# Where the weight sums of three streamed Strassen products are made: in DRAM ahead of each product, or in the product's own SBUF tile

## The chip, the cores and the metric

The kernel runs on one core of a Trainium2 chip. The metric is device microseconds of one execution; before the change the median of three is 1978.28 us (1976.78 to 1981.49). The profile comes from one further execution, which took 1979.15 us, 1977.4 of them from its first to its last instruction.

## The reference

One decoder block on 1024 tokens of width 1024, in float32. Only the middle of it matters here:

```python
def hybrid_mixer(...):
    proj = n @ w_in
    ...
    merged = jax.nn.sigmoid(g_ssd) * (y_ssd @ w_up_ssd) + jax.nn.sigmoid(g_gla) * (y_gla @ w_up_gla)
    return merged @ w_o

def mem_cross_attention(n, m, w_xq, w_xkv, w_xo):
    q = (n @ w_xq).reshape(Bsz, S, XATTN_HEADS, XATTN_HEAD_DIM)
    ...
```

with `h = h + hybrid_mixer(rmsnorm(h, ...))` and then `h = h + mem_cross_attention(rmsnorm(h, ...), ...)`. The three 1024 x 1024 products with w_up_gla, w_o and w_xq follow one another, each needs the one before, and they are the streamed stages of the title.

## The kernel before, in words

**Products.** A float32 operand is split into two float32r parts (ACT rounds the high part, DVE subtracts it: `split`, lines 229 to 235, seen as L234 or, negated, L231 on ACT and as L73 on DVE), and three matmuls of the parts stand for one. Large products are also done by one level of the Strassen-Winograd scheme: seven products of 512 x 512 quadrants in place of eight, called B11, B21, B22 (plain quadrants on the right) and T1 to T4 (sums on both sides).

**The streamed stages** are three objects of class `Wide` (from line 1228): `ug` (w_up_gla), `wo`, `xq`. Each runs `SEQ`, seven products in the order B11, T1, B22, T2, B21, T3, T4. A product has two halves (contraction chunks 0,1 and 2,3) of 24 matmuls each, four PSUM banks for four row groups u. `load` brings the left operand of a product, a tile `wr` of 1 MB, by SP. For B11, B21 and T4 it is a quadrant of the weight; for T1, B22, T2 and T3 it is a sum of quadrants: A21+A22, A12+A11+A21+A22, A11+A21+A22, A11+A21 (A is the transposed weight; the minus signs of the scheme are put on the other side). `prep` makes a half's operands: where needed it combines two quadrants of the input on DVE (`COMB`, in tiles `rq`), then splits the weight half (`ws<-wr`) and the input half (`ws<-rq`). `steps` calls load three products ahead and prep up to two halves ahead, gives the matmuls and then `evac` for the four banks. T2, T3 and T4 add onto the banks of B11 (the `chain`), B22 onto those of T1. `evac` copies or adds the bank into a tile `wk` (for wo: scale and add onto the residual, loaded from `xT_d`), and where the quadrant is complete calls `post`.

**The sums** are made in DRAM by `weight_sums`: for a matrix, twelve transfers on POOL's queue (four copies of 1 MB and eight accumulating transfers of 512 KB), into `ugs_d`, `wos_d` and `xqs_d`, from where `load` fetches them like quadrants. Those of w_up_gla run through the SSD and GLA stages and `dense(0)` (the product with w_up_ssd), those of w_o during ug, those of w_xq during wo. In the last three stages `paced` gives them out by hand-written plans, and holds POOL back by a small copy, `mark`, of the newest result.

**Between the stages.** `post_yg` (ug) multiplies each finished group by its gate into `wo.quad`, a tile `rq`, and adds the group of `ysg_d` (the other half of `merged`) by an accumulating transfer of 256 KB on POOL's queue. `post_wo` stores h1 by SP, writes the scaled group into `xq.quad` on ACT and adds its square to the norm's sum (`s1.take`, tile `ssum`, on POOL or DVE). `xq_side` closes those sums (small matmuls `bank<-ones,ssum` into two more banks). `wide_side(x, n, m)` starts the next stage's loads and first two preps after n and n + m steps of the stage before.

**Order.** A planner orders the instructions of each engine at build time by priority and a model of time; each engine then works through its queue strictly in that order. What is under `pinned` stays in the program's order on its engine. The tiles come from shared pools: `op` has 14 slots of 8 KB a partition, `aux` 4 and `m` 4; a tile's slot is free when its last reader is done.

Of the kernel before, what the change touches and what calls it, by code (L numbers as in the profile page):

```python
# [16 lines left out]
P = 128  # L17
# [61 lines left out]
def block_kernel(ctx: ExitStack, tc: tile.TileContext, t: dict, out: bass.AP):  # L79
# [19 lines left out]
    def dram(name, *shape):  # L99
        return dr.tile(list(shape), F32, name=name, tag=name)  # L100
# [14 lines left out]
    yg_d = dram("yg_d", D, TOK)  # L115
    act_d = dram("act_d", 7 * D_FF // 2, HALF)
    down_d = dram("down_d", 4 * D_FF // 2, HALF)
    wos_d = dram("wos_d", 2 * D, HALF)
    ugs_d = dram("ugs_d", 2 * D, HALF)
    xqs_d = dram("xqs_d", 2 * D, HALF)  # L120
    kT_d = dram("kT_d", D, MEM)
    vm_d = dram("vm_d", MEM, D)
    cs_d = dram("cs_d", P, P)
# [325 lines left out]
    def run(main, *rest, prio=0):  # L449

        owed = [0.0] * len(rest)
        for _ in main:
            for i, (g, rate) in enumerate(rest):
                owed[i] += rate
                while owed[i] >= 1.0:
                    owed[i] -= 1.0
                    with tc.high_priority(offset=prio):
                        next(g, None)

    def waiting(g, n):  # L460
        for _ in range(n):
            yield
        for _ in g:
            yield
# [602 lines left out]
    st2.close()  # L1067
    sp_ = pool("ssd", 1, stack=st3)
    ssd = ssd_steps()

    def dense_sums(*todo):
        return weight_sums([(t[w].rearrange("(j k p) c -> j p k c", j=2, p=P), d, 4, 0) for w, d in todo])

    wsums = dense_sums(("w_up_gla", ugs_d))
    with tc.manual_schedule(engines={mybir.EngineType.PE}):
        run(singles(ru + qk + gs[:2], B, gs[2:3]), (ssd, 80 / 70), (waiting(wsums, 14), 0.25), prio=PRIO)
    drain(ssd)
    st3.close()

# [118 lines left out]
            yield  # L1198

    gla = gla_steps()  # L1200
    run(singles(gs[2:] + gg[:3], B, gg[3:]), (gla, 8 * 5 / 30), (wsums, 0.22), prio=PRIO)
    drain(gla)
    st4.close()
    st_early.close()
# [23 lines left out]
    class Wide:  # L1228
# [1 line left out]

        SEQ = ("B11", "T1", "B22", "T2", "B21", "T3", "T4")
        LEFT = {"B11": (0, 0), "B21": (0, 1), "T1": 0, "B22": 3, "T2": 1, "T3": 2, "T4": (1, 1)}
        COMB = {"T1": (sub, (0, 0), (0, 0), (0, 1)), "T2": (add, (0, 0), (1, 1), (0, 0)),
                "T3": (sub, (0, 1), (1, 1), (0, 1)), "T4": (sub, (1, 0), (0, 0), (1, 0))}
        RIGHT = {"B11": (0, 0), "B22": (1, 1), "B21": (1, 0), "T1": (0, 0), "T2": (0, 0), "T3": (0, 1), "T4": (1, 0)}
        OUT = {"B11": (0, 0), "T1": (1, 1), "B22": (0, 1), "T2": (0, 1), "B21": (0, 0), "T3": (1, 1), "T4": (1, 0)}

        def __init__(s, W, sums_d, post, keys, side, base=None, scale=1.0, two=None):  # L1240
            s.W, s.sums_d, s.post, s.keys, s.side, s.base, s.scale = W, sums_d, post, keys, side, base, scale
            s.two = two or (lambda ap: DVE)
            s.q, s.raw, s.ops, s.keep, s.chain = {}, [], [], {}, None

        def quad(s, i, j):
            if (i, j) not in s.q:
                s.q[i, j] = slot("op", (P, 4, HALF), name="rq")
            return s.q[i, j]

        def load(s, n):  # L1250
            while len(s.raw) < min(n, 7):
                src = s.LEFT[s.SEQ[len(s.raw)]]
                if isinstance(src, tuple):
                    i, j = src
                    w = s.W[half(j), half(i)]
                else:
                    w = s.sums_d[half(src), :]
                r = slot(s.keys[len(s.raw)], (P, 4, HALF), name="wr")
                pinned(SP.dma_start(r, w.rearrange("(k p) c -> p k c", p=P)))
                s.raw.append(r)  # L1260

        def home(s, i, j):
            if (i, j) not in s.keep:
# [5 lines left out]
        def prep(s, n, pin=None):  # L1269
            pin = pin or (lambda x: x)  # L1270
            while len(s.ops) < min(n, 14):
                m, kp = divmod(len(s.ops), 2)
                s.load(m + 1)
                name, c = s.SEQ[m], slice(2 * kp, 2 * kp + 2)
                x = [slot("op", (P, 2, 2, HALF), F32R, name="ws") for _ in range(2)]
                with ahead():
                    if name in s.COMB:
                        f, *q = s.COMB[name]
                        o, a, b = (s.quad(*ij)[:, c] for ij in q)
                        f(s.two(o), o, a, b)  # L1280
                    split(s.raw[m][:, c], x[0][:, 0], x[0][:, 1], pin=pin)
                    split(s.quad(*s.RIGHT[name])[:, c], x[1][:, 0], x[1][:, 1], neg=name == "T2", pin=pin)
                s.ops.append(x)

        def evac(s, name, u, p):
            i, j = s.OUT[name]
            o = p if name == "T4" and s.base is None else s.home(i, j)[:, u]
            if o is not p:
                recent[0] = o
            first = name in ("B11", "T1", "B22")  # L1290
            with ahead():
                if s.base is not None:
                    DVE.scalar_tensor_tensor(o, p, -s.scale if i else s.scale, o, ALU.mult, ALU.add)
                elif first:
                    ACT.activation(o, p, AF.Copy, scale=-1.0 if i else 1.0)
                elif name == "T3":
                    sub(DVE, o, o, p)
                elif name != "T4":
                    add(DVE, o, p, o)
                if not first:  # L1300
                    s.post(i, j, u, o)

        def steps(s):
            x = 0
            for m, name in enumerate(s.SEQ):
                if name in ("B11", "T1", "B21"):
                    banks = [(acc if name == "B11" else bank)() for _ in range(4)]
                    if name == "B11":
                        s.chain = banks
                elif name in ("T2", "T3", "T4"):  # L1310
                    banks = s.chain
                fresh = name in ("B11", "T1", "B21")
                if s.base is not None:
                    for z in s.SEQ[m:m + 2]:
                        s.home(*s.OUT[z])
                for kp in range(2):
                    s.load(m + 3)
                    s.prep(x + 3)
                    w, b = s.ops[x]
                    for u in range(4):  # L1320
                        for k in range(2):
                            for n, (a, c) in enumerate(((0, 0), (0, 1), (1, 0))):
                                PE.matmul(banks[u], w[:, a, k, u * P:(u + 1) * P], b[:, c, k],
                                          start=fresh and kp + k + n == 0, stop=kp + k == 2 and n == 2,
                                          skip_group_check=True)
# [137 lines left out]

    def post_ys(o, j, p, g):
        gated(g, p)
        recent[0] = g
        SP.dma_start(ysg_d[o * P:(o + 1) * P, half(j)], g)

    gg = []
# [19 lines left out]
        fetch_gg(4)  # L1489
        yield  # L1490

    mark = cp.tile([P, 1], F32, name="mark")
    recent = [None]

    def paced(sums, plan):

        for n in plan:
            if n:
                pinned(POOL.tensor_copy(mark, recent[0][:, :1]))
            for _ in range(n):  # L1500
                next(sums, None)
            yield

    ug = Wide(t["w_up_gla"], ugs_d, post_yg, ("aux", "aux") + ("op",) * 5, ("aux",) * 3)

    def post_wo(i, j, u, q):
        o = 4 * i + u
# [1 line left out]
        put_xq(o, j, q, col("norm_xattn", o))  # L1509
        s1.take(j, q)  # L1510

    wo = Wide(t["w_o"], wos_d, post_wo, ("aux",) * 7, ("m", "m", "m", "aux"), xT_d, 0.5)

    def wide_side(x, n, m, pin=None):
        for _ in range(n):
# [16 lines left out]
            stats.take(j, q)  # L1532
        return post

    xq = Wide(t["w_xq"], xqs_d, lambda i, j, u, p: into(i_q, 4 * i + u, j, p, neg=(i, j) == (1, 0)), ("m", "m", "aux", "aux", "m", "aux", "aux"), ("m", "m", "aux"))

    def put_xq(o, j, q, g):
        ACT.activation(xq.quad(o // 4, j)[:, o % 4], q, AF.Copy, scale=g)

    wosums, xqsums = dense_sums(("w_o", wos_d)), dense_sums(("w_xq", xqs_d))  # L1540
    PLAN0 = (0,) * 12 + (1, 1, 0, 0)
    PLAN1 = (2,) + (2, 0) * 3 + (1, 0) * 3 + (1,)
    PLAN2 = (0, 2) * 5 + (0, 1) * 2
    run(dense(0, i_ys, post_ys, lambda o, j: gate(gs_d, o, j)), (fetch_gated(yg_d, sr_d, ug), 1.0),
        (wide_side(ug, 8, 4, pinned), 1.0), (paced(wsums, PLAN0), 1.0))
    drain(wsums)
    fetch_gg(1)
    run(ug.steps(), (yg_side(), 1.0), (wide_side(wo, 9, 2), 1.0), (paced(wosums, PLAN1), 1.0))
    drain(wosums)
    run(wo.steps(), (wide_side(xq, 7, 2), 1.0), (paced(xqsums, PLAN2), 1.0))  # L1550
    drain(xqsums)


    kv = []
# [17 lines left out]
    xsc = cp.tile([P, NCH], F32, name="xsc")  # L1572

    def xq_side():
        for _ in range(2):
            yield
        s1.close(0)
        s1.close(1)
        DVE.tensor_scalar(xsc, s1.r, XSC, None, ALU.mult)
        yield  # L1580
        ex1 = cp.tile([P, 1], F32, name="ex1")
        ACT.activation(ex1, xsc[:, :1], AF.Exp, scale=0.0)
        yield
# [363 lines left out]
```

## Time and profile before

| | |
|---|---|
| median of three | 1978.28 us |
| profiled execution | 1979.15 us (span 1977.4) |
| TensorE busy | 1899.4 us, 96% |
| VectorE (DVE), ScalarE (ACT) busy | 1384.7 us, 895.6 us |
| GpSimd (POOL) busy | 546.4 us |
| mean granted TensorE clock | 0.984 |
| POOL's DMA queue | 52.43 MB |
| the three streamed stages | 896.98 to 1181.08 us |

In the lines below, `wk<-acc,wk` is an instruction that writes wk and reads acc and wk; what stands in square brackets is how long its engine was idle before it and who released it. PE is TensorE's matmuls. SPq and POOLq are the DMA queues of SyncE and GpSimd; a line `POOL ... DMA_DIRECT2D` is the issue of a transfer, and its landing comes later. "issue" as a releaser means that the engine waited for nothing that the profile shows, on POOL mostly for earlier transfers to make room. `L73` and `L51` are helpers that record every elementwise operation and every matmul, so one goes by tile names.

### The profile page before, as it was taken

What the parts mean: (1) busy time and instruction counts of PE and PEld (TensorE: products, weight loads), DVE (VectorE), ACT (ScalarE), POOL (GpSimd) and SP (SyncE); (2) the same over time, 40 slices, a digit from 0 to 9 for tenths busy, and PEclk for the clock granted to TensorE, in tenths of its full rate; (3) what the DMA queues carried; (4) which work ended last, traced back from release to release, by engine and by line L of the source; (5) the groups of instructions that cost most, each with busy time, mean ns of one, the idle gap of its engine ahead of it and who ended that gap; (6) DMA issues with size and microseconds to landing.
All of it is one profiled execution on the core that took longest, in us unless ns stands there. A gap on an engine that the chain in (4) does not pass through costs nothing.

```text
span 1977.4 us, 26044 instructions
## 1 busy us (share of the span) xinstructions
PE 1899.4 (96%) x9632; PEld 1597.6 (81%) x9632; DVE 1384.7 (70%) x1960; ACT 895.6 (45%) x1527; POOL 546.4 (28%) x454
## 2 busy tenths in 40 slices
PE   7999999999999999999679799999999999999998
PEld 7998787888877888788567688888888888888888
DVE  7765879877786665546567577577787887866566
ACT  7535465645552454536225455453333333345243
POOL 0012433354534222001222300006444444430002
PEclk9999999999999999999889899999999999999999
DMA  9423383455647664968788620333666556387463
GB/s 343 135 92 100 138 296 131 149 177 158 188 156 218 193 196 138 377 221 274 184 217 242 193 96 11 107 129 112 169 164 188 145 153 163 120 276 273 160 225 126
DMA packets 246083, 352.57 MB, mean 178 GB/s; under 512 B 16682, under 2 KB 143892, under 8 KB 245956
## 3 DMA queue, kind: packets, MB, share of 16 engines
q1 hardware_dynamic: 223172, 292.18, 43.7%
q0 software_dynamic: 21056, 52.43, 12.7%
q10 hardware_dynamic: 1728, 6.29, 0.8%
q8 instruction: 76, 1.25, 0.3%
q14 instruction: 51, 0.42, 0.1%
HBM read 261.40 MB, written 137.69 MB: 202 GB/s over the span
## 4 chain that ended last, share of the span: by engine, by line
PE 76%; DVE 8%; issue 6%; DMA 5%; POOL 2%; ACT 2%; SPq 0%; POOLq 0%; DVEq 0%; ACTq 0%
PE acc L51 60%; PE bank L51 14%; DVE cv L73 2%; DVE wlo L73 2%; PE bank L55 2%; DVE o L73 1%; POOL ssum L73 1%; DVE ws L73 1%; DMA zr<-sz_d 1%; DMA wr<-wos_d 1%; DMA hl<-ys_d 1%; DVE hs L73 1%; DMA raw<-in_w_in_dram 0%; DMA down_d<-in_w_ffn_out_dram 0%; DMA raw<-in_w_ffn_in_dram 0%
## 5 line engine op out<-in xcount | busy, mean ns | idle before, releaser
L73 DVE TENSOR_TENSOR wlo<-raw,whi 128x512 fp32r<-128x512 f32 x272 | 243.3, 902 | 93.0 <-ACT whi L234 92.9
L234 ACT ACTIVATE whi<-raw 128x512 fp32r<-128x512 f32 x272 | 169.5, 629 | 253.1 <-PE acc L51 206.6
L73 DVE TENSOR_TENSOR o<-acc,o 128x512 f32<-128x512 f32 x244 | 167.0, 685 | 91.3 <-PE acc L51 89.6
L51 PE MATMUL acc<-hl,wd 128*128 128x512 f32 x768 | 179.1, 394 | 4.0 <-ACT wd L234 3.9
L51 PE MATMUL acc<-ws 128*128 128x512 f32 x576 | 142.8, 408 | 34.9 <-DVE wk L73 18.7
L51 PEld LDWEIGHTS acc<-hl,wd 128*128 128x128 f32 x768 | 145.5, 190 | 35.8 <-ACT wd L234 4.9
L51 PEld LDWEIGHTS acc<-ws 128*128 128x128 f32 x576 | 113.9, 199 | 61.7 <-DVE wk L73 15.8
L51 PE MATMUL acc<-fs 128*128 128x512 f32 (+1 forms) x792 | 155.7, 355 | 0.1
L51 PEld LDWEIGHTS acc<-fs 128*128 128x128 f32 x792 | 130.7, 189 | 20.8 <-issue 0.5
L73 DVE TENSOR_TENSOR fs<-fr,fs 128x1024 fp32r<-128x1024 f32 (+1 forms) x78 | 93.0, 1225 | 36.5 <-ACT fs L234 36.1
L234 ACT ACTIVATE fs<-fr 128x1024 fp32r<-128x1024 f32 (+1 forms) x78 | 74.0, 983 | 93.8 <-PE acc L51 29.1
L73 POOL TENSOR_TENSOR sa<-raw 128x512 f32<-128x512 f32 x42 | 66.4, 1582 | 154.5 <-DMA raw<-in_w_in_dram 80.6
L51 PE MATMUL bank<-ws 128*128 128x512 f32 x432 | 102.2, 395 | 6.1 <-DVE wk L73 6.1
L234 ACT ACTIVATE whi<-sa 128x512 fp32r<-128x512 f32 x96 | 59.7, 626 | 98.4 <-PE acc L51 93.0
L51 PEld LDWEIGHTS bank<-ws 128*128 128x128 f32 x432 | 82.5, 191 | 24.0 <-issue 6.5
L73 POOL TENSOR_TENSOR raw<-raw,sa 128x512 f32<-128x512 f32 x32 | 42.5, 1329 | 157.0 <-DVE wlo L73 157.0
L51 PE MATMUL acc<-T4h,whi 128*128 128x512 f32 x192 | 76.4, 398 | 2.6 <-DVE o L73 2.6
L73 POOL TENSOR_TENSOR rstd<-rstd,mhalf 128x4 f32<-128x4 f32 (+1 forms) x7 | 8.7, 1252 | 251.8 <-DVE rstd L73 251.8
L73 DVE TENSOR_TENSOR wlo<-sa,whi 128x512 fp32r<-128x512 f32 x96 | 71.9, 749 | 8.5 <-ACT whi L234 7.6
L51 PE MATMUL acc<-B22h,wlo 128*128 128x512 f32 x192 | 75.6, 394 | 1.5 <-DVE wlo L73 1.5
L51 PE MATMUL acc<-T1h,whi 128*128 128x512 f32 x192 | 76.3, 397 | 0.0
L51 PE MATMUL acc<-T3h,whi 128*128 128x512 f32 x192 | 76.0, 396 | 0.0
(424 smaller groups left out, 5129.9 us busy)
## 6 DMA issues: line engine op xcount, KB each, us to landing
raw<-in_w_in_dram SPq DMA_DIRECT2D x26, 1024.0 KB, 7.8
raw<-in_w_ffn_in_dram SPq DMA_DIRECT2D x22, 1024.0 KB, 8.5
act_d<-o SPq DMA_DIRECT2D x77, 256.0 KB, 2.6
fr<-act_d SPq DMA_DIRECT2D x35, 512.0 KB, 6.0
down_d<-in_w_ffn_out_dram POOLq DMA_DIRECT2D x18, 768.0 KB, 7.3
fr<-down_d SPq DMA_DIRECT2D x20, 512.0 KB
ga<-h_d SPq DMA_DIRECT2D x32, 256.0 KB, 4.7
csb<-cs_d SPq DMA_DIRECT2D x15, 512.0 KB, 4.2
```

The source lines that it names most:

```text
L51: return s.e.matmul(o, x, y, **kw)
L55: return s.e.transpose(o, x, i)
L73: return f(*a, **kw)
L234: pin(ACT.activation(hi, src, AF.Copy))
```

## The change

No sum goes to DRAM. In a stage only five left tiles are loaded (B11, T1, B21, T3, T4), T1 and T3 with the plain quadrant (1,0) or (0,0). The tile of T1 serves three products in turn. `plus` adds a quadrant to it from the weight in HBM, by accumulating transfers on POOL's queue of half a tile (512 KB) each: (1,1) right after the load for T1; (0,0) onto a half as soon as prep has split that half for T1, for T2; (0,1) onto it once it is split for T2, for B22. T3's tile gets (1,0) after its load. So a stage has eight accumulating transfers. For this the order becomes B11, T1, T2, B22, B21, T3, T4; T2 and B22 exchange their places, the first into the tile of quadrant (0,1) is now T2. `load` runs four products ahead, not three (two of the seven need no tile). `weight_sums` stays for the FFN only; `paced`, `mark` and the plans go; wo's first loads follow one another a step sooner, and `xq_side` closes the norm's sums one step earlier.

```diff
-    def dense_sums(*todo):
-        return weight_sums([(t[w].rearrange("(j k p) c -> j p k c", j=2, p=P), d, 4, 0) for w, d in todo])
-
-    wsums = dense_sums(("w_up_gla", ugs_d))
...
-        run(singles(ru + qk + gs[:2], B, gs[2:3]), (ssd, 80 / 70), (waiting(wsums, 14), 0.25), prio=PRIO)
+        run(singles(ru + qk + gs[:2], B, gs[2:3]), (ssd, 80 / 70), prio=PRIO)
...
-    run(singles(gs[2:] + gg[:3], B, gg[3:]), (gla, 8 * 5 / 30), (wsums, 0.22), prio=PRIO)
+    run(singles(gs[2:] + gg[:3], B, gg[3:]), (gla, 8 * 5 / 30), prio=PRIO)
...
-        SEQ = ("B11", "T1", "B22", "T2", "B21", "T3", "T4")
-        LEFT = {"B11": (0, 0), "B21": (0, 1), "T1": 0, "B22": 3, "T2": 1, "T3": 2, "T4": (1, 1)}
+        SEQ = ("B11", "T1", "T2", "B22", "B21", "T3", "T4")
+        LEFT = {"B11": (0, 0), "B21": (0, 1), "T1": (1, 0), "T3": (0, 0), "T4": (1, 1)}
+        PLUS = {"T1": (1, 1), "T2": (0, 0), "B22": (0, 1), "T3": (1, 0)}
...
+        def block(s, i, j):
+            return s.W[half(j), half(i)].rearrange("(k p) c -> p k c", p=P)
+
+        def plus(s, m, c):
+            pinned(POOL.dma_start(s.raw[m][:, c], s.block(*s.PLUS[s.SEQ[m]])[:, c], accum_op=ALU.add))
+
         def load(s, n):
             while len(s.raw) < min(n, 7):
-                src = s.LEFT[s.SEQ[len(s.raw)]]
-                if isinstance(src, tuple):
-                    i, j = src
-                    w = s.W[half(j), half(i)]
-                else:
-                    w = s.sums_d[half(src), :]
-                r = slot(s.keys[len(s.raw)], (P, 4, HALF), name="wr")
-                pinned(SP.dma_start(r, w.rearrange("(k p) c -> p k c", p=P)))
+                m = len(s.raw)
+                name = s.SEQ[m]
+                if name not in s.LEFT:
+                    s.raw.append(s.raw[m - 1])
+                    continue
+                r = slot(next(s.keys), (P, 4, HALF), name="wr")
+                pinned(SP.dma_start(r, s.block(*s.LEFT[name])))
                 s.raw.append(r)
+                if name in s.PLUS:
+                    for k in (0, 2):
+                        s.plus(m, slice(k, k + 2))
...
                     split(s.raw[m][:, c], x[0][:, 0], x[0][:, 1], pin=pin)
                     split(s.quad(*s.RIGHT[name])[:, c], x[1][:, 0], x[1][:, 1], neg=name == "T2", pin=pin)
+                if name in ("T1", "T2"):
+                    s.load(m + 2)
+                    s.plus(m + 1, c)
                 s.ops.append(x)
...
-            first = name in ("B11", "T1", "B22")
+            first = name in ("B11", "T1", "T2")
...
                 if name in ("B11", "T1", "B21"):
-                    banks = [(acc if name == "B11" else bank)() for _ in range(4)]
+                    other = [(acc if name == "B11" else bank)() for _ in range(4)]
                     if name == "B11":
-                        s.chain = banks
-                elif name in ("T2", "T3", "T4"):
-                    banks = s.chain
+                        s.chain = other
+                banks = s.chain if name in ("T2", "T3", "T4") else other
...
-                    s.load(m + 3)
+                    s.load(m + 4)
...
     run(dense(0, i_ys, post_ys, lambda o, j: gate(gs_d, o, j)), (fetch_gated(yg_d, sr_d, ug), 1.0),
-        (wide_side(ug, 8, 4, pinned), 1.0), (paced(wsums, PLAN0), 1.0))
-    drain(wsums)
+        (wide_side(ug, 8, 4, pinned), 1.0))
     fetch_gg(1)
-    run(ug.steps(), (yg_side(), 1.0), (wide_side(wo, 9, 2), 1.0), (paced(wosums, PLAN1), 1.0))
-    drain(wosums)
-    run(wo.steps(), (wide_side(xq, 7, 2), 1.0), (paced(xqsums, PLAN2), 1.0))
-    drain(xqsums)
+    run(ug.steps(), (yg_side(), 1.0), (wide_side(wo, 9, 1), 1.0))
+    run(wo.steps(), (wide_side(xq, 7, 2), 1.0))
...
     def xq_side():
-        for _ in range(2):
-            yield
+        yield
         s1.close(0)
         s1.close(1)
```

More of the change, by code (lines that the diff above doesn't have):

```diff
@@ L117, in block_kernel @@
     down_d = dram("down_d", 4 * D_FF // 2, HALF)
-    wos_d = dram("wos_d", 2 * D, HALF)
-    ugs_d = dram("ugs_d", 2 * D, HALF)
-    xqs_d = dram("xqs_d", 2 * D, HALF)
     kT_d = dram("kT_d", D, MEM)
@@ L1238, in block_kernel, with __init__ @@
         OUT = {"B11": (0, 0), "T1": (1, 1), "B22": (0, 1), "T2": (0, 1), "B21": (0, 0), "T3": (1, 1), "T4": (1, 0)}
-        def __init__(s, W, sums_d, post, keys, side, base=None, scale=1.0, two=None):
-            s.W, s.sums_d, s.post, s.keys, s.side, s.base, s.scale = W, sums_d, post, keys, side, base, scale
+        def __init__(s, W, post, keys, side, base=None, scale=1.0, two=None):
+            s.W, s.post, s.keys, s.side, s.base, s.scale = W, post, iter(keys), side, base, scale
             s.two = two or (lambda ap: DVE)
@@ L1287, in evac @@
             o = p if name == "T4" and s.base is None else s.home(i, j)[:, u]
-            if o is not p:
-                recent[0] = o
-            first = name in ("B11", "T1", "B22")
+            first = name in ("B11", "T1", "T2")
             with ahead():
@@ L1465, in post_ys @@
         gated(g, p)
-        recent[0] = g
         SP.dma_start(ysg_d[o * P:(o + 1) * P, half(j)], g)
@@ L1490, in yg_side @@
         yield
[L1492 to L1501, printed above, removed]
-            yield
-    ug = Wide(t["w_up_gla"], ugs_d, post_yg, ("aux", "aux") + ("op",) * 5, ("aux",) * 3)
+    ug = Wide(t["w_up_gla"], post_yg, ("aux", "aux", "op", "op", "op"), ("aux",) * 3)
     def post_wo(i, j, u, q):
@@ L1510, in post_wo @@
         s1.take(j, q)
-    wo = Wide(t["w_o"], wos_d, post_wo, ("aux",) * 7, ("m", "m", "m", "aux"), xT_d, 0.5)
+    wo = Wide(t["w_o"], post_wo, ("aux",) * 5, ("m", "m", "m", "aux"), xT_d, 0.5)
     def wide_side(x, n, m, pin=None):
@@ L1533, in residual @@
         return post
-    xq = Wide(t["w_xq"], xqs_d, lambda i, j, u, p: into(i_q, 4 * i + u, j, p, neg=(i, j) == (1, 0)), ("m", "m", "aux", "aux", "m", "aux", "aux"), ("m", "m", "aux"))
+    xq = Wide(t["w_xq"], lambda i, j, u, p: into(i_q, 4 * i + u, j, p, neg=(i, j) == (1, 0)), ("m", "m", "aux", "aux", "aux"), ("m", "m", "aux"))
     def put_xq(o, j, q, g):
         ACT.activation(xq.quad(o // 4, j)[:, o % 4], q, AF.Copy, scale=g)
[L1540 to L1543, printed above, removed]
     run(dense(0, i_ys, post_ys, lambda o, j: gate(gs_d, o, j)), (fetch_gated(yg_d, sr_d, ug), 1.0),
-        (wide_side(ug, 8, 4, pinned), 1.0), (paced(wsums, PLAN0), 1.0))
-    drain(wsums)
+        (wide_side(ug, 8, 4, pinned), 1.0))
     fetch_gg(1)
-    run(ug.steps(), (yg_side(), 1.0), (wide_side(wo, 9, 2), 1.0), (paced(wosums, PLAN1), 1.0))
-    drain(wosums)
-    run(wo.steps(), (wide_side(xq, 7, 2), 1.0), (paced(xqsums, PLAN2), 1.0))
-    drain(xqsums)
+    run(ug.steps(), (yg_side(), 1.0), (wide_side(wo, 9, 1), 1.0))
+    run(wo.steps(), (wide_side(xq, 7, 2), 1.0))
     kv = []
@@ L1574, in xq_side @@
     def xq_side():
-        for _ in range(2):
-            yield
+        yield
         s1.close(0)
```

## The prediction, made before the changed kernel ran

> **What bounds the kernel now.** I read the page's slices first, then the window of the three streamed stages, then in that window the waits of TensorE, its timeline and the chain, last the POOL queue. The slices:
>
> ```profile
> span 1977.4 us, 26044 instructions
> ...
> PE   7999999999999999999679799999999999999998
> ...
> PEclk9999999999999999999889899999999999999999
> ```
>
> TensorE is full nearly everywhere; the one hole inside the span lies in slices 20 to 24, where the granted clock falls too. That is where the three streamed products run (up_gla, then w_o, then w_xq):
>
> ```profile
> core 0: us, PE busy (x) PEld busy (x) DVE busy (x) ACT busy (x) POOL busy (x), PEclk, DMA share, GB/s
> 896.98:1181.08 284.10, 243.07 (x1026) 198.33 (x1025) 183.62 (x203) 128.27 (x164) 64.96 (x66) 0.92 0.71 202
> ```
>
> ```profile
> L51 PE MATMUL acc<-ws 128*128 128x512 f32 x576 | 142.8, 408 | 34.9 <-DVE wk L73 18.7 <-ACT ws L231 11.6 <-DVE ws L73 4.5
> ...
> L51 PE MATMUL bank<-ws 128*128 128x512 f32 x432 | 102.2, 395 | 6.1 <-DVE wk L73 6.1
> ```
>
> 1008 matmuls in 284.1 us. What they need comes from a stretch without gaps in the timeline of PE (the first two lines), and the gaps from the others:
>
> ```profile
> 907.86 11.04 PE L51 MATMUL bank<-ws 128*128 128x512 f32 x48
> 918.74 1.07 PE L51 MATMUL acc<-ws 128*128 128x512 f32 x4
> ...
> 984.40 8.75 PE L51 MATMUL acc<-ws 128*128 128x512 f32 x25 [15.17 <-DVE wk L73]
> ...
> 998.58 6.71 PE L51 MATMUL acc<-ws 128*128 128x512 f32 x17 [4.52 <-DVE ws L73]
> ...
> 1026.86 13.29 PE L51 MATMUL bank<-ws 128*128 128x512 f32 x48 [6.14 <-DVE wk L73]
> ...
> 1076.28 15.30 PE L51 MATMUL acc<-ws 128*128 128x512 f32 x60 [3.48 <-DVE wk L73]
> 1091.42 1.07 PE L51 MATMUL bank<-ws 128*128 128x512 f32 x4
> ...
> 1122.20 6.41 PE L51 MATMUL acc<-ws 128*128 128x512 f32 x16 [11.58 <-ACT ws L231]
> ...
> 1140.24 1.84 PE L51 MATMUL bank<-ones,ssum 128*128 128x1 f32 x16
> ```
>
> 48 matmuls take 918.74 - 907.86 = 10.88 us, 0.2267 each, so a product (48) is 10.88 us, one of its two halves 5.44 us, a stage of seven products 76.2 us. 1008 x 0.2267 = 228.5, with 1.7 for the small sums 230.2. **Lost: 284.1 - 230.2 = 53.9 us.** The five gaps are 15.17 + 4.52 + 6.14 + 3.48 + 11.58 = 40.9; the other 13.0 is slow clock behind them (25 matmuls in 8.75 us at 984.4, where 5.7 would do), 0.32 us for each us of gap.
>
> Who is behind the gaps? The chain, in order of time:
>
> ```profile
> 1010.12 5.72 DMA wos_d<-wos_d
> ...
> 1017.08 12.33 DMA wr<-wos_d
> ...
> 1105.17 5.43 DMA xqs_d<-xqs_d
> ...
> 1110.66 5.67 DMA wr<-xqs_d
> ```
>
> The last sum of w_o lands in DRAM at 1015.8, is loaded back until 1029.4, and only then split: that is the 6.14 gap. The same with w_xq is the 11.58 gap. The 15.17 and 4.52 have another way (POOL, then DVE and ACT):
>
> ```profile
> 956.41 0.69 DVE L73 SCALAR_TENSOR_TENSOR rq<-gg,wk 128x512 f32<-128x512 f32 x1
> ...
> 982.52 1.22 DVE L73 TENSOR_TENSOR ws<-rq,ws 128x1024 fp32r<-128x1024 f32 x1 [19.75 <-ACT ws L234]
> ```
>
> ```profile
> 981.43 1.06 ACT L234 ACTIVATE ws<-rq 128x1024 fp32r<-128x1024 f32 x1 [28.78 <-DMA rq<-ysg_d]
> ```
>
> ```profile
> 959.03 2.69 POOL L73 DMA_DIRECT2D rq<-ysg_d  x3 [3.97 <-issue]
> ...
> 967.14 1.17 POOL L73 DMA_DIRECT2D wos_d<-in_w_o_dram  x1 [4.95 <-issue]
> 968.80 0.93 POOL L73 DMA_DIRECT2D rq<-ysg_d  x1 [0.48 <-issue]
> 976.60 1.75 POOL L73 DMA_DIRECT2D rq<-ysg_d  x2 [6.88 <-issue]
> ```
>
> DVE had finished quadrant (0,0) of w_o's input at 957.1. Its four additions of ysg_d stand in POOL's queue behind a weight sum and issue from 968.8 to 979. ACT waits for them, DVE waits for ACT, and behind that waiting split on DVE stands the evacuation that TensorE needs for T4. POOL's queue passes one 512 KB transfer, or three of 256 KB, in about 6 to 8 us.
>
> **The change, part by part.** *Removed:* 36 sum transfers on POOL (12 a matrix), 6 loads of 1 MB on SP (T2 and B22 of each matrix), the mark copies. *Added:* 24 accumulating transfers of 512 KB on POOL, HBM into the tile. Their price has no row; the nearest are
>
> ```profile
> rq<-ysg_d POOLq DMA_DIRECT2D x16, 256.0 KB, 6.0
> ...
> wos_d<-in_w_o_dram POOLq DMA_DIRECT2D x6, 512.0 KB, 7.0
> ...
> xqs_d<-xqs_d POOLq DMA_DIRECT2D x2, 512.0 KB, 5.3
> ```
>
> ```profile
> DMA to landing us min/median/max: 4.0/6.0/9.6
> ```
>
> (the last line is that of the ysg additions, which also go from DRAM into SBUF). I take 6.5 us, issue to landing and issue to issue, between 5.3 and 7.0 as a size for size match; 9.6 is the far end. The Trainium skill, "DMA: Bandwidth & Descriptors", section "Anatomy of one DMA", fits POOL's transfers by 2.0 us plus bytes over 436 GB/s; for 512 KB an estimate of 3.2 us. The rows of this trace show about twice that. By 3.2 the term below for w_o's chain would be nothing and the sum 8 us lower.
>
> *up_gla.* ACT and DVE split T1's halves here ahead of TensorE, while dense(0) still holds the slots:
>
> ```profile
> 895.59 1.05 ACT L234 ACTIVATE ws<-wr 128x1024 fp32r<-128x1024 f32 x1
> ```
>
> ```profile
> L73 DVE TENSOR_TENSOR ws<-wr,ws x42: 1216/1219/1708, 867.2 to 1159.0; 128x1024 fp32r<-128x1024 f32 x42
> ```
>
> A split is 1.05 on ACT and 1.22 on DVE, 2.3 us. T2's first half can be added at about 899, landed 905.5, and is needed at 897 + 4 x 5.44 = 918.8; the four chained additions end at 899 + 4 x 6.5 = 925 and the last is needed at 897 + 7 x 5.44 = 935. Cost 0; the cover is 8 to 13 us. Swapping B22 and T2 keeps the banks of T1 over one more product, and lets T1's evacuation take a product longer: 0.
>
> *up_gla to w_o.* Without sums in between, the four additions of (0,0) issue by 958, land by 964, two splits later (969) w_o's B11 is ready, before TensorE is through with up_gla at 897 + 76.2 = 973. 15.17 and 4.52 go. Next late: the evacuation of T4, 1 us.
>
> *w_o.* Here POOL is behind. After (0,0) it issues T1's two additions (967.5, 974), then eight of ysg_d at three per 6 us (until 989), and only then T2's first half: landed 995.5, split 998, needed at 973 + 21.8 = 994.8: 3 us of gap. After it each addition takes 6.5 against TensorE's 5.44: about 1 us for each of the next three. 6 us; at 5.3 it is 2, at 7.0 it is 8. In this wait DVE and ACT stand at the split, with B11's evacuation behind. The 6.14 goes; T3 to T4 stays as it is (3.48, an evacuation behind splits).
>
> *w_xq.* T1's block is loaded during w_o, POOL has only the ssum additions besides: the chain fits and the 11.58 goes. New: the sums of squares are closed one step earlier, so two PSUM banks for them are taken before T1's four. T1 waits until ssum is complete and read. The last addition before was
>
> ```profile
> 1103.50 0.69 DVE L73 TENSOR_TENSOR ssum<-ssum,sq 128x512 f32<-128x512 f32 x1 [2.72 <-POOL ssum L73]
> ```
>
> w_o's T4 is 48 of the 60 matmuls that start at 1076.28 (15.1 us until the next row of PE), so it ends at 1088.4; ssum is complete 15.8 later, and with the small matmuls (1.84 in the row at 1140) that is 17.6 against 10.88 for B11: 7 us, if T4's evacuations stand behind splits on DVE as they did. I take 4, between 0 and 8. POOL's ssum additions also queue behind T2's transfer.
>
> *Earlier stages.* Up_gla's sums no longer run there:
>
> ```profile
> 540.00:807.00 267.00, 258.27 (x1364) 216.95 (x1363) 174.38 (x323) 123.67 (x276) 75.97 (x67) 1.00 0.63 192
> ```
>
> TensorE is idle 8.7 us in these 267, mostly at stage borders which stay; a gain of 2, between -2 (another order of the planner) and 5.
>
> *SP.* Two loads a matrix fewer, the rest issued a product earlier: 0, there is slot room since two tiles a matrix are gone. If the early load blocked the queue, the loads of w_o's base and the h1 stores would stand behind it (rival 2).
>
> **Sum.** Gaps left: 1 + 6 + 3.5 + 4 = 14.5, with 0.32 each for the clock 19.1. Gain 53.9 - 19.1 + 2 = 36.8. The profiled execution took 1979.15 us (span 1977.4), the median is 1978.28, 0.9 lower: 1979.15 - 36.8 - 0.9 = **1941 us**. With all unknowns at their good ends (gaps of 1 + 2 + 3.5, times 1.32, 5 early) 1929; at their bad ends (1 + 8 + 3.5 + 8, -2) 1953.
>
> **Rivals.** (1) *All hidden.* A transfer takes less than TensorE's 5.44 us a half and POOL is never behind, T1 of w_xq finds its banks, and the 3.48 goes too: 1978.3 - 53.9 - 3 = 1921. For it: POOL has less to move, and the shortest median of 512 KB was 5.3; against: DVE is busy 183.6 of 230, and its bursts made the 3.48. Chance 0.14. The skill's fit, cited above, would lead here.
>
> (2) *POOL's queue still holds up the border.* T1's additions for w_o stand in the program before the ysg additions of (1,1) and (1,0), and wait for a load that waits for a slot of up_gla. If that load comes at 970, they issue at 977 and 984, T2's right side and sum come 10 us later; with clock 13 us more here, and the like at w_xq: 1941 + 13 to 26 = 1954 to 1967. For it, in SP's queue, the load of w_o's T1:
>
> ```profile
> 962.22 0.37 SPq L1259 DMA_DIRECT2D wr<-wos_d  x1
> ```
>
> so late before, but then it had a sum to wait for too. Chance 0.17.
>
> (3) *Slower: the chain of additions becomes the bound.* T1's tile is now read, added to, read, added to, four transfers in a row for its two halves with nothing to run ahead. From the stage's start TensorE comes to B22's second half after 7 x 5.44 = 38.1 us; two splits (4.6) and four transfers fit if one takes under 8.4 us. Above, each us costs 4 in a stage, 12 in three, 16 with the clock; all 53.9 is eaten at 8.4 + 3.4 = 11.8 us. At 13 us it would be 1978 + 20 = 1998. For it: the ysg additions took up to 9.6 us for half the bytes; against: their median is 6.0 and those into DRAM, which read and write HBM for the sum as well, took 7.0. Chance 0.10.
>
> (4) *No change.* The price lies just at that point, or the planner gives back as much in the later stages: 1978. Chance 0.04.
>
> Against the change also speaks the skill's page named above, section "Issuing engine by pattern": plain loads belong on SP, which is generally faster, and POOL is for what only it can do. Here two loads of SP a matrix give way to POOL's; no run shows them side by side yet.
>
> **How the numbers follow.** Forecast 0.55, rivals 0.14, 0.17, 0.10, 0.04. Faster by more than 0.2% (4 us, about what a measurement of this kernel can tell): 0.55 + 0.14 + 0.17 = 0.86; within: 0.04; slower: 0.10. The range goes from rival 1's 1921 to the end of rival 2, 1967; outside lie rivals 3 and 4 and the tails of the others.
>
> **What would show it.** Right: the window of the three stages shrinks from 284 to some 247 us; the gaps at 984, 998, 1027 and 1122 have no successors at those steps; POOL's additions land in 5 to 7 us; the gaps left stand at T2 of w_o (released by a wr addition, over ACT and DVE) and at T1 of w_xq (released by ssum or the closing). Wrong: additions of 9 us and more; gaps at T2 or B22 in all three stages; the ysg additions late again; or a gain over 45 us, which would mean that w_o's queue and w_xq's banks cost nothing.

## The result, and the profile after

The changed kernel takes 1953.37 us (median of 4, 1951.89 to 1954.52) against 1979.88 for the kernel before beside it (4 runs, 1976.78 to 1981.78): ratio 0.9867, 95% interval 0.985 to 0.9884. It is faster by 26 us, within the range, 12 us short of the 1941 forecast. The profiled execution took 1953.51.

The page of the changed kernel, span, TensorE's slices and clock:

```profile
span 1951.8 us, 26021 instructions
...
PE   7999999999999999999888999999999999999998
...
PEclk9999999999999999999989999999999999999999
```

The hole is shallower, not closed. The window of the three streamed stages (first matmul of ug to the first after xq), and the two groups of matmuls in it:

```profile
core 0: us, PE busy (x) PEld busy (x) DVE busy (x) ACT busy (x) POOL busy (x), PEclk, DMA share, GB/s
888.87:1155.88 267.01, 241.57 (x1025) 195.90 (x1024) 182.48 (x203) 127.24 (x164) 57.25 (x49) 0.96 0.69 171
```

```profile
L51 PE MATMUL acc<-ws 128*128 128x512 f32 x576 | 138.6, 401 | 13.9 <-DVE rq L73 7.7 <-DVE wk L73 3.4 <-ACT ws L228 2.1
...
L51 PE MATMUL bank<-ws 128*128 128x512 f32 x432 | 104.7, 399 | 11.5 <-DVE wk L73 6.2 <-ACT ws L231 2.6 <-ACT wk L1297 1.4
```

Two things to see. The window starts 8.1 us earlier (888.87, before 896.98), so the stages ahead of it got shorter; and it lasts 267.0 us where 284.1 were, against a need of 230.2: 36.8 us are still lost, 25.4 in gaps (13.9 + 11.5) and 11.4 to matmuls that run slower than 0.2267 us (the granted clock is 0.96 in the window). 8.1 + 17.1 = 25.2 of the 25.6 us by which the span shrank. Where the gaps are, from TensorE's timeline:

```profile
943.84 21.92 PE L51 MATMUL acc<-ws 128*128 128x512 f32 x96
968.36 1.20 PE L51 MATMUL bank<-ws 128*128 128x512 f32 x4 [2.59 <-ACT ws L231]
969.39 2.89 PE L51 MATMUL acc<-ws 128*128 128x512 f32 x12
979.94 5.17 PE L51 MATMUL acc<-ws 128*128 128x512 f32 x12 [7.66 <-DVE rq L73]
...
1002.62 1.20 PE L51 MATMUL acc<-ws 128*128 128x512 f32 x4 [2.07 <-ACT ws L228]
1004.67 11.88 PE L51 MATMUL acc<-ws 128*128 128x512 f32 x44 [0.85 <-DVE ws L73]
...
1033.72 13.73 PE L51 MATMUL bank<-ws 128*128 128x512 f32 x48 [4.39 <-DVE wk L73]
...
1075.33 10.06 PE L51 MATMUL acc<-ws 128*128 128x512 f32 x36 [3.36 <-DVE wk L73]
```

ug runs with one gap of 0.29 (888.87 to 965.6, 76.7 us for a need of 76.2). At the start of wo stand 2.59 and 7.66; at T2 and B22 of wo 2.07, 0.85 and two small ones (4.2 together); then 4.39 at B21, 3.36 at the start of xq, and 2.9 inside xq. What is behind the 2.59 and the 7.66, in POOL's queue, on ACT and on DVE:

```profile
921.81 1.21 POOL L73 DMA_DIRECT2D wr<-in_w_up_gla_dram  x1 [5.38 <-PE acc L51]
928.48 1.21 POOL L73 DMA_DIRECT2D wr<-in_w_up_gla_dram  x1 [5.47 <-issue]
...
959.85 1.20 POOL L73 DMA_DIRECT2D wr<-in_w_o_dram  x1 [6.41 <-issue]
966.57 1.22 POOL L73 DMA_DIRECT2D wr<-in_w_o_dram  x1 [5.51 <-issue]
967.30 1.43 POOL L73 DMA_DIRECT2D rq<-ysg_d  x1
973.64 2.67 POOL L73 DMA_DIRECT2D rq<-ysg_d  x3 [4.91 <-issue]
```

```profile
966.30 1.06 ACT L231 ACTIVATE ws<-wr 128x1024 fp32r<-128x1024 f32 x1 [3.99 <-DMA wr<-in_w_o_dram]
```

```profile
978.06 1.23 DVE L73 TENSOR_TENSOR rq<-rq 128x1024 f32<-128x1024 f32 x1 [8.31 <-DMA rq<-ysg_d]
979.20 0.68 DVE L73 SCALAR_TENSOR_TENSOR rq<-gg,acc 128x512 f32<-128x512 f32 x1
```

One addition into a weight tile follows the other 6.6 to 6.7 us later (928.48 - 921.81, 966.57 - 959.85): POOL passes one at a time and sits idle some 5.4 us in between. The 2.59 is a wait for T1's own first addition: the planner put four matmuls of wo's T1 ahead of B11, and the half that they need landed at 966.3. The 7.66 is another matter. The two additions for wo's T1 go ahead of the ysg additions of quadrant (1,1); DVE, in its strict order, waits for those with the sum for T2, and the evacuation `rq<-gg,acc` of ug's T4, whose bank TensorE needs, stands right behind.

### The profile page after: what moved, and what is told of

Same layout as the page of the kernel before. It is cut to its first block, busy times and chain, and to the rows that moved or that the text cites. A ratio compares the mean times of both kernels' runs of the same rounds, so it can differ in the third digit from the quotient of the medians.

```text
span 1951.8 us, 26021 instructions
## 1 busy us (share of the span) xinstructions
PE 1893.5 (97%) x9632; PEld 1591.2 (82%) x9632; DVE 1376.0 (71%) x1953; ACT 896.3 (46%) x1527; POOL 536.6 (27%) x432
## 4 chain that ended last, share of the span: by engine, by line
PE 74%; DVE 9%; issue 7%; DMA 5%; POOL 2%; ACT 2%; SPq 0%; POOLq 0%; DVEq 0%; ACTq 0%
PE acc L51 60%; PE bank L51 13%; DVE cv L73 2%; DVE wlo L73 2%; PE bank L55 2%; DVE o L73 1%; DVE hs L73 1%; DMA wr<-in_w_xq_dram 1%; DVE ws L73 1%; DMA zr<-sz_d 1%; POOL ssum L73 1%; POOL rq L73 0%; DMA hl<-ys_d 0%; ACT ws L231 0%; DMA wr<-in_w_up_gla_dram 0%
## 5 line engine op out<-in xcount | busy, mean ns | idle before, releaser
L73 DVE TENSOR_TENSOR wlo<-raw,whi 128x512 fp32r<-128x512 f32 x272 | 247.5, 918 | 101.3 <-ACT whi L231 100.4
L51 PE MATMUL acc<-ws 128*128 128x512 f32 x576 | 138.6, 401 | 13.9 <-DVE rq L73 7.7
L51 PE MATMUL bank<-ws 128*128 128x512 f32 x432 | 104.7, 399 | 11.5 <-DVE wk L73 6.2
L73 POOL TENSOR_TENSOR raw<-raw,sa 128x512 f32<-128x512 f32 x35 | 46.8, 1339 | 170.6 <-DVE wlo L73 170.6
L73 DVE TENSOR_TENSOR ws<-wr,ws 128x1024 fp32r<-128x1024 f32 x42 | 52.6, 1251 | 57.1 <-ACT ws L231 57.1
L231 ACT ACTIVATE ws<-wr 128x1024 fp32r<-128x1024 f32 x42 | 44.2, 1052 | 88.6 <-PE bank L51 25.1
L51 PE MATMUL acc<-T1h,whi 128*128 128x512 f32 x192 | 76.2, 397 | 0.0
```

Source lines behind the costliest of these rows:

```text
L51: return s.e.matmul(o, x, y, **kw)
L73: return f(*a, **kw)
L231: pin(ACT.activation(hi, src, AF.Copy))
```

## Experiments

Every kernel below has four or five executions, beside the kernel before; the table gives their median, and the ratio to the kernel before. "Start" is the first matmul of ug, "window" as above, "lost" the window less 230.2; the three come from the timelines.

| kernel | median us | ratio (95%) | start | window | lost |
|---|---|---|---|---|---|
| before | 1978 to 1981 | 1 | 897.0 | 284.1 | 53.9 |
| changed | 1953.4 | 0.9867 (0.985 to 0.9884) | 888.9 | 267.0 | 36.8 |
| e1 changed + dead DRAM sums | 1963.5 | 0.9925 (0.9912 to 0.9938) | 899.1 | 267.8 | 37.6 |
| e11 the same, SSD stage alone | 1954.8 | 0.9877 (0.9856 to 0.9898) | 890.0 | 265.9 | 35.7 |
| e2 before + new order | 1963.7 | 0.9914 (0.9898 to 0.9929) | 896.2 | 270.8 | 40.6 |
| e8b before + 256 KB | 1958.4 | 0.9893 (0.9876 to 0.991) | 894.3 | 267.1 | 36.9 |
| e9 before + new order + 256 KB | 1954.3 | 0.9878 (0.9856 to 0.9899) | 898.3 | 260.6 | 30.4 |
| e3 changed, T1 behind ysg (1,1) | 1951.5 | 0.9864 (0.9851 to 0.9878) | 886.8 | 266.6 | 36.4 |
| e4 changed, ysg off POOL | 1933.7 | 0.9777 (0.9763 to 0.979) | 887.3 | 248.9 | 18.7 |
| e5 changed, 256 KB | 1926.3 | 0.9738 (0.9725 to 0.9751) | 889.7 | 241.4 | 11.1 |
| e6 e4 and e5 together | 1919.7 | 0.9694 (0.968 to 0.9708) | 887.8 | 234.1 | 3.9 |
| e7 changed, 128 KB | 1939.9 | 0.9798 (0.9783 to 0.9812) | 888.2 | 255.5 | 25.3 |
| e10 changed, 256 KB in 256 rows | 2012.1 | 1.0166 (1.0146 to 1.0185) | 885.9 | 328.4 | 98.2 |

**Where do the earlier 8 us come from? (e1, e11)** e1 puts the sums of w_up_gla back into SSD and GLA; nothing reads them.

```diff
+    ugs_d = dram("ugs_d", 2 * D, HALF)
...
+    wsums = weight_sums([(t["w_up_gla"].rearrange("(j k p) c -> j p k c", j=2, p=P), ugs_d, 4, 0)])
...
-        run(singles(ru + qk + gs[:2], B, gs[2:3]), (ssd, 80 / 70), prio=PRIO)
+        run(singles(ru + qk + gs[:2], B, gs[2:3]), (ssd, 80 / 70), (waiting(wsums, 14), 0.25), prio=PRIO)
...
-    run(singles(gs[2:] + gg[:3], B, gg[3:]), (gla, 8 * 5 / 30), prio=PRIO)
+    run(singles(gs[2:] + gg[:3], B, gg[3:]), (gla, 8 * 5 / 30), (wsums, 0.22), prio=PRIO)
```

> The changed kernel, with the DRAM sums of w_up_gla put back into the SSD and GLA stages where they were; nothing reads them. Theory (the 8 us by which the first streamed stage starts earlier come from POOL's queue and the DMA engines being free of these sums): 1959 to 1963 us, stage starts near 896. Rival (the planner only happened on a better order there): 1952 to 1955, stage starts near 889.

1963.5 us (half a us above the theory's range), start at 899.1, the window as in the changed kernel: the theory. The loss is on both sides of the GLA stage. The stretch from 600 to 660 us, first the changed kernel, then e1:

```profile
600.00:660.00 60.00, 59.90 (x300) 49.76 (x299) 43.72 (x77) 21.49 (x43) 21.63 (x20) 1.00 0.57 185
```

```profile
600.00:660.00 60.00, 56.21 (x282) 46.38 (x282) 40.88 (x69) 19.79 (x36) 21.75 (x20) 1.00 0.81 234
```

3.7 us of TensorE are lost here, and one more from 540 to 600. The DMA engines are busier in e1 (0.81 in place of 0.57), but what TensorE waits for is POOL's order: a sum's issue waits 3.81 us for DVE, POOL's small operation on `rs` stands behind it, and TensorE needs `rs`.

```profile
620.09 1.19 POOL L73 DMA_DIRECT2D ugs_d<-in_w_up_gla_dram  x1 [3.81 <-DVE wlo L73]
620.84 1.05 POOL L73 TENSOR_TENSOR rs<-rs,mhalf 128x1 f32<-128x1 f32 x1
```

```profile
621.93 0.49 PE L51 MATMUL bank<-ident,rs 128*128 128x128 f32 x2 [2.58 <-POOL rs L73]
```

The other 1.2 of the 3.7 is a wait for DVE (`qk`) near 648. The changed kernel has neither wait, the kernel before has both (1.6 and 1.1 us). Of the rest of the 9.2 us by which `dense(0)` starts later (810.20 against 800.98), some 2.5 are lost at the end of the GLA stage, where its inputs are loaded and split (a wait of 3.36 in e1, 0.9 in the changed kernel):

```profile
810.20 89.06 PE L51 MATMUL acc<-hl,wd 128*128 128x512 f32 x384 [3.36 <-ACT wd L232]
```

e11 takes the `(wsums, 0.22)` out again.

> The changed kernel with dead DRAM sums of w_up_gla in the SSD stage alone, not in the GLA stage (with both it was 1963.5, without 1953.4). Theory (most of the 10 us is lost where the GLA stage ends and w_up_ssd's inputs are loaded beside the last sums): 1953 to 1957. Rival (it is lost in the SSD stage, where POOL's arithmetic stands behind the issues): 1960 to 1964.

1954.8: as expected, but it says less than it was meant to. Only three of e1's ten transfers run in it (594 to 611 us). Those three cost nothing that can be told from the changed kernel (the intervals overlap); the other seven, issued from 620 to 790 in e1, cost the rest, and not at the end alone. The first of the seven is the one at 620.09 above, so that 2.6 us of the loss are POOL's order, the rival's mechanism. For the end of the GLA stage, the DMA engines and POOL's order were not separated.

**Is it the sums' place or the order? (e2)** The kernel before, with T2 ahead of B22 and the banks that go with it, the sums still in DRAM.

```diff
-        SEQ = ("B11", "T1", "B22", "T2", "B21", "T3", "T4")
+        SEQ = ("B11", "T1", "T2", "B22", "B21", "T3", "T4")
...
-            first = name in ("B11", "T1", "B22")
+            first = name in ("B11", "T1", "T2")
...
-                    banks = [(acc if name == "B11" else bank)() for _ in range(4)]
+                    other = [(acc if name == "B11" else bank)() for _ in range(4)]
...
+                banks = s.chain if name in ("T2", "T3", "T4") else other
```

> The kernel before, with only the order of the products changed (T2 ahead of B22, with its banks); the sums still go through DRAM. Theory (the gain comes from the sums leaving DRAM and POOL, the order gives nothing by itself): 1975 to 1981. Rival (T2's sum is ready one transfer earlier in DRAM than B22's, so the order alone takes 5 us and more out of the gaps of 6.1 and 11.6): 1966 to 1973.

1963.7: my theory falls, the rival holds and more. The window shrinks by 13.3 us. Its gaps:

```profile
983.04 8.37 PE L51 MATMUL acc<-ws 128*128 128x512 f32 x25 [14.64 <-DVE wk L73]
...
999.32 6.92 PE L51 MATMUL acc<-ws 128*128 128x512 f32 x17 [7.00 <-DVE ws L73]
...
1074.46 16.66 PE L51 MATMUL acc<-ws 128*128 128x512 f32 x60 [9.28 <-DVE wk L73]
```

The 6.14 and the 11.58 of before are gone: the last sum in DRAM is B22's, and B22 is now wanted a product (10.9 us) later. The gap at wo's start is as it was (14.64 and 7.00 for 15.17 and 4.52), and the 3.48 before wo's T4 has grown to 9.28. So 17 us can be had from the order alone, with every sum still made in DRAM; the whole change brings 26.

**What holds wo back in the changed kernel? (e3, e4)** e3 changes one number, `wide_side(wo, 9, 1)` to `wide_side(wo, 9, 2)`, and so puts T1's two additions behind the ysg additions of (1,1).

> The changed kernel, with w_o's T1 load and its two additions one step later in the program, behind the ysg additions of quadrant (1,1). Theory (the 7.7 us gap at w_o's start is the order of POOL's queue: T1's additions ahead of those of (1,1), which DVE waits for in front of up_gla's last evacuations): that gap goes, T1 waits 2 to 4 us instead, 1945 to 1950 us. Rival (POOL is simply full from 890 to 1033, any order gives the same): 1952 to 1956, the gap moves to T1.

1951.5, between the two ranges, and not to be told from the changed kernel (the intervals overlap). The gaps decide:

```profile
966.37 5.51 PE L51 MATMUL acc<-ws 128*128 128x512 f32 x23 [1.33 <-DVE ws L73]
973.56 4.38 PE L51 MATMUL acc<-ws 128*128 128x512 f32 x18 [1.68 <-DVE rq L73]
...
997.20 13.43 PE L51 MATMUL acc<-ws 128*128 128x512 f32 x48 [6.25 <-ACT ws L228]
```

The 7.66 shrinks to 1.33 and 1.68, but T2 then waits 6.25 in place of 2.07, and xq starts with 6.43 in place of 3.36. That is the rival, the queue is full in any order, though the gap moved to T2 and not to T1. e4 takes the sixteen ysg additions off it:

```diff
-        pinned(POOL.dma_start(q, ysg_d[(4 * i + u) * P:(4 * i + u + 1) * P, half(j)], accum_op=ALU.add))
+        add(DVE, q, q, quad(ysg_d, (4 * i + u) * P, 0, j))
```

> The changed kernel, with the 16 ysg additions taken off POOL's queue: SP loads each group into a spare tile and DVE adds it (16 additions more on DVE, 11 us of its time in a stage where it is busy 50 of 76). Theory (POOL's queue is the bound from up_gla's middle to the middle of w_o): the gaps of 2.6 and 7.7 at w_o's start and the 4.2 at its T2 and B22 go, with their slow clock 15 to 20 us: 1933 to 1940 us. Rival (DVE's strict order is the bound, and it gets more work): 1950 to 1960.

1933.7: the theory, though one gap of 3.14 stays at B22 of wo. POOL now has time: ahead of the first addition for T1 and the first for T2 it waits 20.13 and 10.71 us for DVE, and between the two of T1 for its own transfer:

```profile
949.00 1.21 POOL L73 DMA_DIRECT2D wr<-in_w_o_dram  x1 [20.13 <-DVE ws L73]
955.68 1.22 POOL L73 DMA_DIRECT2D wr<-in_w_o_dram  x1 [5.47 <-DMA wr<-in_w_o_dram]
967.62 1.21 POOL L73 DMA_DIRECT2D wr<-in_w_o_dram  x1 [10.71 <-DVE ws L73]
```

**Is it the bytes, or the queue? (e5, e10, e7)** e5 cuts each accumulating transfer in two, one chunk (128 rows of 2 KB, 256 KB) each:

```diff
-            pinned(POOL.dma_start(s.raw[m][:, c], s.block(*s.PLUS[s.SEQ[m]])[:, c], accum_op=ALU.add))
+            for k in range(c.start, c.stop):
+                pinned(POOL.dma_start(s.raw[m][:, k], s.block(*s.PLUS[s.SEQ[m]])[:, k], accum_op=ALU.add))
```

> The changed kernel, with each accumulating transfer into a weight tile cut in two of 256 KB. Theory (a 512 KB transfer holds POOL's queue for 6.6 us because only one fits at a time; of 256 KB three are in flight): the pair passes in 4 to 5 us, w_o's chain keeps up, 1940 to 1948 us. Rival (the 6.6 us are the bytes' own time): 1952 to 1957, a pair still takes 6.6 or a little more.

1926.3, better than the theory's best. In POOL's queue:

```profile
908.36 0.87 POOL L73 DMA_DIRECT2D wr<-in_w_up_gla_dram  x1 [2.06 <-DVE ws L73]
909.43 0.89 POOL L73 DMA_DIRECT2D wr<-in_w_up_gla_dram  x1 [0.20 <-issue]
910.74 0.88 POOL L73 DMA_DIRECT2D wr<-in_w_up_gla_dram  x1 [0.42 <-PE bank L51]
913.17 0.87 POOL L73 DMA_DIRECT2D wr<-in_w_up_gla_dram  x1 [1.54 <-issue]
914.96 0.87 POOL L73 DMA_DIRECT2D wr<-in_w_up_gla_dram  x1 [0.92 <-issue]
916.24 0.89 POOL L73 DMA_DIRECT2D wr<-in_w_up_gla_dram  x1 [0.40 <-issue]
```

Six transfers are issued in 7.9 us (908.36 to 916.24), five steps of 1.6: a pair passes in 3.2 us where the same 512 KB in one took 6.6. The bytes alone do not set that time. e10 makes the same 256 KB out of both chunks and half the columns, 256 rows of 1 KB:

```diff
+            for h in (slice(0, HALF // 2), slice(HALF // 2, HALF)):
+                pinned(POOL.dma_start(s.raw[m][:, c, h], s.block(*s.PLUS[s.SEQ[m]])[:, c, h], accum_op=ALU.add))
```

> The changed kernel with each accumulating transfer cut in two of 256 KB the other way: both chunks, half the columns, so 256 rows of 1 KB where the cut by chunks has 128 rows of 2 KB. Theory (POOL's queue holds a number of rows, not of bytes: 256 rows of a 512 KB transfer block it, three transfers of 128 rows go together): one in flight again, twice as many, 1955 to 1985. Rival (bytes count): as the cut by chunks, 1925 to 1931.

2012.1 us, slower than the kernel before and beyond the theory's range, in its direction:

```profile
904.34 1.21 POOL L73 DMA_DIRECT2D wr<-in_w_up_gla_dram  x1 [5.80 <-issue]
908.81 1.21 POOL L73 DMA_DIRECT2D wr<-in_w_up_gla_dram  x1 [3.26 <-issue]
913.31 1.21 POOL L73 DMA_DIRECT2D wr<-in_w_up_gla_dram  x1 [3.29 <-issue]
917.74 1.22 POOL L73 DMA_DIRECT2D wr<-in_w_up_gla_dram  x1 [3.22 <-issue]
```

One at a time again, every 4.5 us, 8.9 for 512 KB, and TensorE now has gaps at T2 or B22 in all three stages. Equal bytes, opposite results: a transfer of 256 rows has POOL's queue to itself, of those with 128 rows several are on the way. e7 cuts to 128 KB (128 rows of 1 KB).

> The changed kernel with accumulating transfers of 128 KB (one chunk, half its columns, rows of 1 KB). Theory (what counted was that more than one transfer is in flight; from 256 KB on the issue, 0.87 us each, is the price): 1926 to 1935, not better than 256 KB. Rival (the more in flight the better): 1918 to 1923.

1939.9: slower than 256 KB, as the theory had it, by more than it said. Four transfers of 128 rows take the place of two, and again only a few pass at a time:

```profile
889.92 2.69 POOL L73 DMA_DIRECT2D wr<-in_w_up_gla_dram  x3 [26.49 <-DVE ws L73]
898.34 0.89 POOL L73 DMA_DIRECT2D wr<-in_w_up_gla_dram  x1 [5.72 <-issue]
899.73 2.81 POOL L73 DMA_DIRECT2D wr<-in_w_up_gla_dram  x3 [0.50 <-issue]
907.77 2.69 POOL L73 DMA_DIRECT2D wr<-in_w_up_gla_dram  x3 [5.23 <-issue]
```

**Size without place (e8b, e9).** The kernel before, with the additions of weight quadrants in `weight_sums` cut to 256 KB (not the copies, not the last addition of each matrix); e9 has e2's order besides.

```diff
-                    if more:
+                    if more and kn == 4 and at < 7:
+                        for k in range(c.start, c.stop):
+                            pinned(POOL.dma_start(o[:, k], a[:, k], accum_op=ALU.add))
+                    elif more:
```

> The kernel before, with the additions of weight quadrants in its DRAM sums cut into 256 KB (three of four additions of each matrix; copies and the last addition stay). Theory (the round trip through DRAM is a cost of its own: a sum lands, is loaded, then split): some of the 15 and 4.5 us gaps go, the 6.1 and 11.6 stay, 1960 to 1972. Rival (the size of the transfers was the whole trouble, in place or not): 1940 to 1955. Second rival (in DRAM the size does not matter): 1976 to 1981.

1958.4: just below the theory's range. Size helps in DRAM too, 22 us, most of it at wo's start (5.09 and 3.81 in place of 15.17 and 4.52) and at xq (2.50 and 1.00 in place of 11.58). The 6.14 stays, as expected (6.99); the 11.58 was expected to stay too.

> The kernel before, with both the new order of the products and the additions of weight quadrants in DRAM cut to 256 KB: the nearest that the DRAM way comes to the changed kernel cut to 256 KB (1926). Theory (sums in place are worth something by themselves: no sums beside SSD and GLA, 8 to 10 us, no round trip through DRAM): 1942 to 1954. Rival (order and size are all of it): 1930 to 1938.

1954.3, at the theory's upper end, and far from the rival. Order and size overlap in DRAM (17 and 22 us alone, 24 together). With order and size equal, sums in place are worth 10 us at 512 KB (1963.7 to 1953.4), about what the early stages give, and 28 at 256 KB (1954.3 to 1926.3). That 28 is not the place alone: e9 still has the copies of 1 MB and the last additions whole in POOL's queue, and e5 has neither.

**Both (e6).** e4's and e5's edits together.

> The changed kernel with both: accumulating transfers of 256 KB, and the ysg additions by SP and DVE. Theory (after the cut POOL's queue is short of time only at T2 of w_o, where 5 us are left; taking ysg off it gives those back): 1919 to 1923. Rival (the cut made the queue free enough, the 16 additions more on DVE now cost): 1927 to 1933.

1919.7, the theory, and the fastest of all: 0.9694 of the kernel before. The window needs 230.2 and takes 234.1:

```profile
887.79:1121.87 234.08, 231.35 (x1025) 190.65 (x1024) 196.12 (x215) 127.13 (x164) 63.70 (x58) 1.00 0.70 188
```

## Why the prediction was right, and where it was wrong

**Right: what there was to win, and who held it.** 53.9 us lost in the window; e6 gets 50 of them. The price of a transfer, taken as 6.5 us, was 6.6 from issue to issue, and POOL's queue was the bound from ug's end to wo's middle, as the term for wo had it: the first addition for T2 issued at 990.95 (989 in the working). ug hides its chain (0 forecast, 76.7 for 76.2 measured). Rival 3, the chain as a bound from 8.4 us a transfer on, did not come to pass at 6.6. e10, at 8.9 us for a half's two, has the gaps that rival 3 names, at T2 or B22 in all three stages, but not its price: by 16 us for each us above 8.4 it would lose 8, and its window loses 61 more than the changed kernel's. The additions also hold up what stands behind them in POOL's queue (4.16 and 7.35 at wo's start), and that was no part of rival 3's sum.

**Right by luck in part: T2 and B22 of wo, 6 forecast, 4.2 measured.** The first addition for T2 took 9.5 us, not 6.5, as the next issue, which waited for it, shows:

```profile
990.95 1.20 POOL L73 DMA_DIRECT2D wr<-in_w_o_dram  x1 [5.16 <-issue]
1000.82 1.22 POOL L73 DMA_DIRECT2D wr<-in_w_o_dram  x1 [8.66 <-DMA wr<-in_w_o_dram]
```

It did little harm, since TensorE, held up at wo's start, came to T2 only at 1000.55 and not at 994.8. In e3, where the start cost less and that addition took 6.4 us, the gap at T2 alone was 6.25.

**Wrong: ug to wo, 1 us forecast, 10.25 measured** (2.59 + 7.66). The 7.66 has the order named in rival 2, T1's additions ahead of those of (1,1). But the load that rival 2 blamed was not late: SP issued it before 946. The additions were late by POOL's own pace, and e3 shows that another order only moves the wait. The step that failed is that I asked only when the operands of wo's B11 would be ready; I did not follow DVE's strict order, in which the sum for T2 waits for (1,1) ahead of ug's last evacuations. The same working gave 989 for the end of the ysg additions, so that the wait could have been read from it. The 2.59 is T1's own first half, landed at 966.3 (an issue at 967.5 in the working): I had B11 go first, and the planner put four matmuls of T1 ahead of it.

**Wrong: the smaller gaps.** T1 of xq did not wait for the banks of the norm's sums (4 forecast, 0); 3.36 came at xq's B11 instead (wo's last evacuations), 2.9 further in. The 3.48 before T4 of wo went, 4.39 came at B21. Together 8.5 forecast with the border's 1, 20.9 measured with its 10.25.

**Mis-sized: the clock.** 0.32 us for each us of gap; it was 11.4 / 25.4 = 0.45, and so 11.4 for 4.6. Over the traces of the table it runs from 0.30 (e2, four gaps, 31.3 us) to 0.73 (e5, five gaps, 6.5 us), mostly low where the gaps are few and long; e3, with eleven gaps and 0.37, does not fit. No run was made for it, and what sets it stays open.

**Mis-sized: the earlier stages.** 2 (between -2 and 5) forecast, 8.1 measured; e1 loses 10 again. The working looked at TensorE's idle time, 8.7 in that stretch, and took most of it for stage borders which stay. They did not stay: the waits for `rs` and `qk` (1.6 and 1.1 us) are gone in the changed kernel, and the one at the start of `dense(0)` fell from 3.4 to 0.9. And 2.0 of the 8.1 lie in `dense(0)` itself, 89.9 us from its start to ug's before and 87.9 after, which the working did not look at.

Sum: 36.8 left in the window where 19.1 was forecast, 17.7 too few; 6.1 more ahead of it; 1941 + 17.7 - 6.1 = 1952.6, measured 1953.4.

**Wrong without showing in the sum: the order.** "Swapping B22 and T2 ...: 0" was wrong. e2 shows 17 us for it alone. The changed kernel cannot do without it, so the total does not tell; but the reason given for the gain, that the round trip through DRAM ends, was at 512 KB nearly all order and early stages. In the window e2 takes 270.8 and the changed kernel 267.0.

**Slips that change nothing.** The load ending at 1029.4 is not behind the 6.14: TensorE went on at 1026.86, before it. That load is T2's. B22's had been issued just ahead of it and was there by 1021.5, when ACT splits it; the evacuation that TensorE needed stands behind those splits on DVE:

```profile
1021.53 1.06 ACT L234 ACTIVATE ws<-wr 128x1024 fp32r<-128x1024 f32 x1 [17.90 <-DMA wr<-wos_d]
```

```profile
1026.03 0.68 DVE L73 SCALAR_TENSOR_TENSOR wk<-bank,wk 128x512 f32<-128x512 f32 x1
```

The way through DRAM is the cause all the same. The good end of the sum is 1928, not 1929, and rival 1's last 3 us have no term: the 3.48 is already in the 53.9.

**The size of a transfer**, which the working left at 512 KB, was worth as much as the change: 27 us gained by halving it (e5), and half of that lost again at 128 KB (e7). The Trainium skill, on its page "DMA: Bandwidth & Descriptors", asks in "Rules for kernel authors" for at least 1 MiB a transfer for maximum bandwidth. For these additions on POOL's queue the smaller of two sizes was the faster: 256 KB every 1.6 us (e5), 512 KB every 6.6; 1 MiB was not run. The fit of the Trainium skill on the same page, in "Anatomy of one DMA", gives an estimate of 3.2 us for 512 KB. One such addition took 6.4 us to land here (median of 24).

## What to carry to other kernels

Ask of a queue not only what a transfer costs but how many it lets be on the way: here halving the transfers did as much for the kernel as the whole change. When several things change in one edit, price the order of the work by itself; moving a product behind the one whose input is ready sooner was worth 17 us in e2. And follow what an in-order engine has queued behind each wait, in the order of the program, down to the evacuation that frees the next bank.

## What the runs showed of the hardware that was not expected

An accumulating transfer of 256 rows from HBM into SBUF on POOL's queue is on the way alone: 512 KB (rows of 2 KB) every 6.6 us, each 6.4 us from issue to landing; 256 KB (rows of 1 KB) every 4.5 us, each 4.2 us to landing (medians). Of those with 128 rows three are issued back to back (128 KB in e7), and 256 KB follow each other at 1.6 us while each takes 5.6 us to land (e5). That it is the number of rows which the queue holds is inferred from these four shapes; nothing in the profile shows the queue's room itself. All kernels here are built with `dynamic_dma_scratch_size=1024`; no run has another value, so whether that sets the room is not shown.
